# Block sums of the MLPs' second weights: by VectorE from SBUF tiles, or by adding transfers in HBM

## The chip, the core and the metric

One core of a Trainium2 chip runs the whole program. The metric is the device time of one execution in microseconds. The engines are TensorE (PE, and PEld for its weight loads), VectorE (DVE), ScalarE (ACT), GpSimd (POOL) and SyncE (SP); sixteen DMA engines serve the transfers that SP and GpSimd issue.

## What is computed

A decoder trunk of two layers over 512 tokens of width 1024, all in fp32. Layer 0 mixes tokens with a Mamba-2 SSD mixer, layer 1 with HGRN2. After each mixer stand a LayerNorm, an MLP with squared ReLU, a second LayerNorm and a gated per-layer input:

```python
h = layer_norm(ALPHA * x + mix, ln_g[i, 0], ln_b[i, 0])
h = layer_norm(ALPHA * h + sq_relu_mlp(h, w1[i], w2[i]), ln_g[i, 1], ln_b[i, 1])
x = h + sigmoid(h @ ple_w_gate[i]) * (p[i] @ ple_w_proj[i])

def sq_relu_mlp(h, w1, w2):
    a = relu(h @ w1)
    return (a * a) @ w2          # 512x1024 @ 1024x4096, 512x4096 @ 4096x1024
```

## The kernel before

**Split products.** Every fp32 factor is split in two parts, hi and lo, and `mm3` issues three matmuls per product (L120, L121, L122). A weight tile of 512 KB, 128 rows of 1024 columns, is a unit. `unit` loads it on SP's queue into one of three `raw` buffers (L106) and calls `split`: ScalarE casts it into one of six `whi` buffers (L113), and VectorE subtracts that into one of six `wlo` buffers (L116). A raw buffer comes free after L116, a whi and a wlo buffer when TensorE has used them.

**The start.** Eight slots, each a piece of x and of the first weights (512 KB), are loaded first (L161). ScalarE and VectorE split them (L167 to L172), and TensorE takes slot after slot, twelve 512-column matmuls each (L749, then L120 to L122).

**The mixers.** In the SSD mixer (to about 355 us of the span) sixteen pairs of heads each project two weight units; `xz` ends with a Silu on ScalarE (L849). `core` loads rows of cumulated decays from a small HBM tensor, csd (L855), makes a matrix of decays of them (L888 to L892), and TensorE uses it in `diagonal` (L906). The HGRN2 mixer lies at about 820 to 1005 us; its `qf` makes a sigmoid per head on ScalarE (L1074).

**The MLPs.** The hidden units of one MLP come in four groups of 1024. `hidden` computes a group: each step T of a period is a projection by one unit of w1, and `half_blocks` (L300) makes from the result a 2x2 grid of blocks and four signed sums of them, each split in hi and lo. `block_product` multiplies the grid with the 2x2 grid of w2's blocks in seven products in place of eight (Strassen's scheme): three take a plain block of w2, four take a sum t1 to t4 of blocks. Each product is a step Q of a period: two units, 24 matmuls, then a drain of the PSUM banks into `acc` by VectorE (L373 to L379). PERIODS (L32) is the order of T and Q.

**The sums of w2's blocks.** `weight_sums` loads blocks of w2 on GpSimd's queue into eight `r` buffers (L329), and VectorE adds and subtracts them in place (L336 to L344): t3 is d - b, t1 is b - a, t2 is t3 + a, t4 is c - t2, with blocks a, b, c, d. `split` then works on the r tiles. The layer's value and gate projections (`values4`) use the same function for other weights, and the last gate (`last_gate`) already makes its sums with copies and adding transfers into SBUF on GpSimd's queue (L401 to L408).

**Order.** The Tile framework's scheduler orders each engine's instructions by priority and dependence; a lead (LEAD, SUMS) moves a load forward. On each engine, and on each queue, instructions then stand in one fixed row: what waits holds up all behind it. GpSimd does little besides the loads of r and a few memsets.

Of the kernel before, what the change touches and what calls it, by code (L numbers as in the profile page):

```python
# [32 lines left out]
SUMS = (60, 300, 300, 300)  # L33
# [11 lines left out]
def trunk(ctx: ExitStack, tc, a):  # L45
# [184 lines left out]

    def transpose_split(src, dst, c, apart, keep=None):
# [68 lines left out]
    def half_blocks(blk, z0, z1, p):  # L300
# [46 lines left out]
    def block_product(w, blk, lead, first, after=None, turns=None, sums=None, low=None):  # L347

        t1, t2, t3, t4 = weight_sums(w, lead, after=low)
# [3 lines left out]
        def product(x, f, name, start, i, j, turns=None):  # L355
            us = [split(v) if f in (t1, t2, t3, t4) else unit(v) for v in f]
# [3 lines left out]
            for c in range(2):  # L360
# [10 lines left out]
                with tc.high_priority(offset=SOON if after else 0):  # L371
                    if after and f in (w[1][0], t1, t4, w[1][1]):
                        nc.vector.tensor_tensor_reduce(  # L373
                            d, ps, d, 1.0, 0.0, ALU.add, ALU.add, sums[:, 2 - 2 * i + c, j : j + 1]
                        )
# [182 lines left out]
    def mlp_and_gate(layer, h_s, last):  # L558
# [36 lines left out]
        for g, period in enumerate(PERIODS):  # L595
            if g < 4:
                tiles = hidden(g)
            if g > 0:
# [10 lines left out]
                products = block_product(w, blocks.pop(g - 1), SUMS[g - 1], g == 1, *((after, turned(0), sums) if g == 4 else ()), low=low if g == 1 else None)  # L609
# [5 lines left out]

        x_n = Split(8)
# [25 lines left out]
        for h in range(2):  # L642
            pu = unit(a[f"wp_{layer}"][h])
            gu = [unit(a[f"wg_{layer}"][4 * h + j]) for j in range(4)]
            for c in range(NCH):
# [17 lines left out]
                nc.scalar.activation(sg, pg, AF.Sigmoid)  # L663
# [6 lines left out]
        return x_n, rows, late  # L670
# [170 lines left out]
    def xz(j):  # L841
        ps = projected(10 * (j // 4) + 2 + 2 * (j % 4))
        xs = tmp("xs", [P, T])
        conv_silu(ps, j, xs)
        if j == 1:
            toks.extend(dt_tail())
        ps = projected(10 * (j // 4) + 3 + 2 * (j % 4))
        sz = tmp("sz", [P, T])
        nc.scalar.activation(sz, ps, AF.Silu)  # L849
        return xs, sz  # L850
# [112 lines left out]

    pend = None
# [41 lines left out]
    x_s, rows, late = mlp_and_gate(0, h_s, False)  # L1006
# [53 lines left out]
    def qf(h):  # L1060
# [13 lines left out]
        nc.scalar.activation(f, ps[1], AF.Sigmoid)  # L1074
# [389 lines left out]
```

## Time and profile before

| | |
|---|---|
| median of 3 runs | 1412.2 us (1411.4 to 1412.49) |
| span of the profiled execution | 1409.6 us |
| what the median has beside the span | 2.6 us |
| TensorE busy | 1404.3 us |
| VectorE busy | 1069.1 us |
| ScalarE busy | 763.6 us |
| moved by DMA | 181.69 MB, 129 GB/s in the mean |

The profiled execution's own time is not listed apart from its span. A row of a window gives, for each engine, busy us and the count of its instructions, then the clock granted to TensorE, the mean busy share of the sixteen DMA engines and GB/s. A row of a wait view gives engine, line and what ended the wait, then the sum of us, the count and the longest. A row of a timeline gives start, duration, engine, line, operation and tiles, and in brackets the idle time before it. A row of DMA issues gives a count, KB each and the median us from issue to landing.

### The profile page before, as it was taken

The page shows a single profiled execution, that of the slowest core. Times are in us where ns is not written, and L with a number is a line of the kernel's source. Part 1 is how long each engine was busy: PE and PEld are TensorE (multiplying, and loading weights), DVE is VectorE, ACT ScalarE, POOL GpSimd, SP SyncE. Part 2 cuts the span into 40 slices and gives each one's busy share as a digit, 9 for nine tenths or more (in the row PEclk, how much of TensorE's full clock was granted, in tenths as well). Part 3 has the DMA queues.
Part 4 walks back from the last instruction along what each step waited for, and adds up shares of the span by engine and source line. Part 5 has one row for each costly group of instructions (what it writes and reads, how often), then busy time and mean ns, then how long its engine had stood idle before and what let it go on. Part 6 is the DMA issues. An engine that isn't in the chain of part 4 may idle for free.

```text
span 1409.6 us, 20400 instructions
## 1 busy us (share of the span) xinstructions
PE 1404.3 (100%) x8001; PEld 1168.1 (83%) x8001; DVE 1069.1 (76%) x1778; ACT 763.6 (54%) x1156; POOL 45.8 (3%) x92
## 2 busy tenths in 40 slices
PE   9999999999999999999999999999999999999998
PEld 7888888888988888888888888888898888888887
DVE  7989688698977668677986577678785867667795
ACT  7766465573354444545555547655555454544573
POOL 0000000001000000000000000000100000000100
PEclk9999999999999999999999999999999999999999
DMA  8433333234433444345621421222443444444731
GB/s 313 135 117 120 106 120 110 85 100 156 141 113 127 157 131 152 129 142 178 209 90 49 134 91 61 76 87 96 150 135 105 147 137 148 144 137 159 202 106 60
DMA packets 50399, 181.69 MB, mean 129 GB/s; under 512 B 5632, under 2 KB 6400, under 8 KB 50176
## 3 DMA queue, kind: packets, MB, share of 16 engines
q1 hardware_dynamic: 38784, 138.45, 29.6%
q0 software_dynamic: 11520, 41.95, 9.2%
q8 instruction: 63, 1.03, 0.3%
q14 instruction: 32, 0.26, 0.1%
HBM read 177.16 MB, written 2.16 MB: 127 GB/s over the span
## 4 chain that ended last, share of the span: by engine, by line
PE 99%; DMA 0%; DVE 0%; issue 0%; DVEq 0%
PE pj L120 25%; PE pj L121 25%; PE pj L122 25%; PE py L120 5%; PE py L122 5%; PE py L121 5%; PE py L906 1%; PE pt L238 1%; PE py L1175 1%; PE pm L923 1%; PE pm L871 1%; PE py L1301 1%; PE pt L859 0%; PE py L1303 0%; PE py L1240 0%; PE py L832 0%
## 5 line engine op out<-in xcount | busy, mean ns | idle before, releaser
L113 ACT CAST whi<-raw 128x1024 fp32r<-128x1024 f32 x218 | 228.8, 1050 | 333.2 <-PE pj L121 243.6
L120 PE MATMUL pj<-b,whi 128*128 128x512 f32 (+1 forms) x990 | 378.6, 383 | 0.0
L122 PE MATMUL pj<-b,wlo 128*128 128x512 f32 (+1 forms) x990 | 376.8, 381 | 0.0
L121 PE MATMUL pj<-b,whi 128*128 128x512 f32 (+1 forms) x990 | 376.6, 381 | 0.0
L116 DVE TENSOR_TENSOR wlo<-raw,whi 128x1024 fp32r<-128x1024 f32 x218 | 265.4, 1221 | 129.4 <-ACT whi L113 128.2
L121 PEld LDWEIGHTS pj<-b,whi 128*128 128x128 f32 x990 | 186.4, 188 | 34.6 <-issue 0.9
L122 PEld LDWEIGHTS pj<-b,wlo 128*128 128x128 f32 x990 | 186.3, 188 | 34.5
L120 PEld LDWEIGHTS pj<-b,whi 128*128 128x128 f32 x990 | 186.1, 188 | 34.0
L122 PE MATMUL pj<-whi,b 128*128 128x512 f32 x520 | 204.1, 392 | 0.0
L120 PE MATMUL pj<-whi,b 128*128 128x512 f32 x508 | 202.1, 398 | 0.0
L121 PE MATMUL pj<-wlo,b 128*128 128x512 f32 x508 | 199.2, 392 | 0.0
L113 ACT CAST whi<-r 128x1024 fp32r<-128x1024 f32 x76 | 80.0, 1053 | 68.5 <-PE pj L122 39.4
L122 PEld LDWEIGHTS pj<-whi,b 128*128 128x128 f32 x520 | 97.7, 188 | 20.1
L120 PEld LDWEIGHTS pj<-whi,b 128*128 128x128 f32 x508 | 95.5, 188 | 19.1 <-ACT b L1322 0.3
L121 PEld LDWEIGHTS pj<-wlo,b 128*128 128x128 f32 x508 | 95.5, 188 | 18.7 <-issue 0.2
L116 DVE TENSOR_TENSOR wlo<-r,whi 128x1024 fp32r<-128x1024 f32 x76 | 92.5, 1220 | 19.6 <-ACT whi L113 19.1
L122 PE MATMUL py<-whi,b 128*128 128x512 f32 x260 | 101.3, 390 | 0.0
L121 PE MATMUL py<-wlo,b 128*128 128x512 f32 x248 | 96.6, 389 | 0.0
L120 PE MATMUL py<-whi,b 128*128 128x512 f32 x248 | 96.4, 390 | 0.0
L329 POOL DMA_DIRECT2D r<-in_w x64 | 34.0, 532 | 1098.8 <-DVE wlo L116 544.3
L122 PEld LDWEIGHTS py<-whi,b 128*128 128x128 f32 x260 | 48.8, 188 | 10.2
L800 DVE SCALAR_TENSOR_TENSOR cv<-pj,cst,cv 128x509 f32<-128x509 f32 (+2 forms) x66 | 48.9, 746 | 10.6 <-ACT cv L797 9.8
(368 smaller groups left out, 1943.5 us busy)
## 6 DMA issues: line engine op xcount, KB each, us to landing
raw<-in_w SPq DMA_DIRECT2D x112, 512.0 KB, 3.3
r<-in_w POOLq DMA_DIRECT2D x64, 512.0 KB, 3.8
raw<-in_wssd SPq DMA_DIRECT2D x36, 512.0 KB, 3.9
a<-csd SPq DMA_DIRECT2D x16, 512.0 KB, 4.1
raw<-in_wso SPq DMA_DIRECT2D x16, 512.0 KB, 3.3
raw<-in_whq SPq DMA_DIRECT2D x16, 512.0 KB, 3.4
raw<-in_wg SPq DMA_DIRECT2D x15, 512.0 KB, 4.0
raw<-in_whvg SPq DMA_DIRECT2D x14, 512.0 KB, 3.4
```

The source lines that it names most:

```text
L113: nc.scalar.copy(hi[:, :n], f)
L116: nc.vector.tensor_sub(lo[:, :n], f, f32(hi[:, :n]))
L120: nc.tensor.matmul(out, sh, mh, start=start, stop=False, **kw)
L121: nc.tensor.matmul(out, sh, ml, start=False, stop=False, **kw)
L122: return nc.tensor.matmul(out, sl, mh, start=False, stop=stop, **kw)
L238: nc.tensor.transpose(pt[:, j * P : (j + 1) * P], src[:, k * P : (k + 1) * P], ident)
L329: queue.dma_start(t[i][u], src)
L800: nc.vector.scalar_tensor_tensor(cv[:, d:], ps[:, : T - d], convw[:, i, k : k + 1], cv[:, d:], ALU.mult, ALU.add)
L871: nc.tensor.matmul(pst_[:, c * P : (c + 1) * P], btok[:, c, :], xw[:, c].rearrange("p h q -> p (h q)"), start=True, stop=True)
L906: mm = nc.tensor.matmul(yds[0][64 * r : 64 * r + 64, sl], xdt[:, 2 * c + r, :], m[:, r, sl], start=True, stop=True)
L923: mm = nc.tensor.matmul(yo[:, c * P : (c + 1) * P], pv[:, c - 1].rearrange("p h q -> p (h q)"), cm[:, c * P : (c + 1) * P], start=True, st ...
L1175: nc.tensor.matmul(pcs[r][bs, at : at + n], kk[r][:, ts], qs, start=True, stop=True)
```

## The change

The sums of w2's blocks are no longer made by VectorE. Two HBM tensors, s2_0 and s2_1, hold them. `mlp_sums` has 16 steps per layer, four per group, each of two transfers of 1 MB on GpSimd's queue; a transfer is a copy or an add onto what lies in the destination. `start_sums` issues one step behind a given ScalarE instruction: the first transfer of a step gets a dependence on it, the second has only those of its data. For layer 0 the steps hang on the 16 Silus of `xz`, for layer 1 on the 8 sigmoids of layer 0's gate and the 8 of `qf`. `block_product` loads the sums with `unit`, like plain weights. As a transfer can add but not subtract, t1, t2, t3 and t4 become plain sums, and signs move into `half_blocks` and into the drains.

```diff
-SUMS = (60, 300, 300, 300)
...
+    def mlp_sums(layer):
+        w, s = a[f"w2_{layer}"], a[f"s2_{layer}"]
+        rows = lambda v: v.rearrange("u p n -> (u p) n")
+        for g in range(4):
+            wa, wb, wc, wd = (rows(w[8 * g + 2 * i : 8 * g + 2 * i + 2]) for i in range(4))
+            t1, t2, t3, t4 = (rows(s[8 * g + 2 * i : 8 * g + 2 * i + 2]) for i in range(4))
+            yield [(t1, wb, False), (t3, wb, False)]
+            yield [(t1, wa, True), (t3, wd, True)]
+            yield [(t2, t3, False), (t2, wa, True)]
+            yield [(t4, t2, False), (t4, wc, True)]
+
+    def start_sums(steps, ins):
+        for n, (out, src, add) in enumerate(next(steps, ())):
+            dma = nc.gpsimd.dma_start(out, src, accum_op=ALU.add, max_dma_last_dim=8192) if add else nc.gpsimd.dma_start(out, src)
+            if n == 0:
+                tc.add_manual_dep(
+                    dma.ins, ins.ins.name, mybir.DependencyInfo(mybir.DependencyClass.Sync, mybir.DependencyReason.DATA), reason="pace"
+                )
...
-        nc.vector.tensor_add(a22, a21, a22)
+        nc.vector.tensor_sub(a22, a22, a21)
         put("a12", a12)
         nc.vector.tensor_sub(a21, a11, a21)
-        nc.vector.tensor_sub(a11, a22, a11)
-        nc.vector.tensor_sub(a12, a12, a11)
+        nc.vector.scalar_tensor_tensor(a11, a22, -1.0, a11, ALU.mult, ALU.subtract)
+        nc.vector.scalar_tensor_tensor(a12, a12, -1.0, a11, ALU.mult, ALU.subtract)
...
-        t1, t2, t3, t4 = weight_sums(w, lead, after=low)
+        t1, t2, t3, t4 = t
...
-            us = [split(v) if f in (t1, t2, t3, t4) else unit(v) for v in f]
+            us = [unit(v) for v in f]
...
+                    op = ALU.subtract if j else ALU.add
+                    if after and x in ("a12", "s1", "a22", "s4"):
+                        sm_ = sums[:, 2 - 2 * i + c, j : j + 1]
+                        if j:
+                            nc.vector.scalar_tensor_tensor(d, ps, -1.0, d, ALU.mult, ALU.add, accum_out=sm_)
+                        else:
+                            nc.vector.tensor_tensor_reduce(d, ps, d, 1.0, 0.0, ALU.add, ALU.add, sm_)
                     elif (i, j) in seen:
-                        nc.vector.tensor_add(d, ps, d)
+                        nc.vector.tensor_tensor(d, d, ps, op)
                     else:
-                        nc.vector.scalar_tensor_tensor(d, d, ALPHA, ps, ALU.mult, ALU.add)
+                        nc.vector.scalar_tensor_tensor(d, d, ALPHA, ps, ALU.mult, op)
...
+                t = [[a[f"s2_{layer}"][8 * g - 8 + 2 * i + u] for u in range(2)] for i in range(4)]
...
+        steps = mlp_sums(1)
...
-                nc.scalar.activation(sg, pg, AF.Sigmoid)
+                start_sums(steps, nc.scalar.activation(sg, pg, AF.Sigmoid))
...
-        nc.scalar.activation(sz, ps, AF.Silu)
+        start_sums(steps, nc.scalar.activation(sz, ps, AF.Silu))
...
+    steps = mlp_sums(0)
...
-        nc.scalar.activation(f, ps[1], AF.Sigmoid)
+        start_sums(steps, nc.scalar.activation(f, ps[1], AF.Sigmoid))
...
+    for i in range(2):
+        args[f"s2_{i}"] = nc.dram_tensor(f"s2_{i}", (32, P, D), F32).ap()
```

**GpSimd's queue at the start of the program**, before: memsets, then the loads of the first MLP's blocks into r tiles (in_w2_0 is w2 of layer 0).

```order
L187 MEMSET one_23_169 128x1
L189 MEMSET ones_s_24_171 128x64
L329 DMA r_665_3840<-in_w2_0 128x1024
L329 DMA r_659_3834<-in_w2_0 128x1024
L329 DMA r_661_3836<-in_w2_0 128x1024
L329 DMA r_666_3841<-in_w2_0 128x1024
```

The same place now, with the semaphores that each waits for (Activation is ScalarE's, DMASW those of transfers on GpSimd's own queue; 16x16384 is a copy in 16 pieces of 64 KB, 128x2048 an add in 128 pieces of 8 KB):

```order
L188 MEMSET ones_s_24_171 128x64
L245 DMA s2_0<-in_w2_0 16x16384 x2
L245 DMA s2_0<-in_w2_0 16x16384 [waits Activation_49]
L245 DMA s2_0<-in_w2_0 128x2048 [waits DMASW0_49]
L245 DMA s2_0<-in_w2_0 128x2048 [waits DMASW2_49,Activation_49]
L245 DMA s2_0<-s2_0 16x16384 [waits DMASW3_49,Activation_49]
```

Two copies, second transfers of two steps, stand right behind the memsets without a wait; the third transfer is the first that waits for a Silu.

**GpSimd's queue around layer 0's gate and the entry to HGRN2**, before: the last loads for values4, then memsets of two tiles of scores.

```order
L329 DMA r_1074_6342<-in_whvg 128x1024
L329 DMA r_1076_6344<-in_whvg 128x1024
L329 DMA r_1077_6345<-in_whvg 128x1024
L329 DMA r_1078_6346<-in_whvg 128x1024
L1022 MEMSET sc_1132_6662 128x512
L1022 MEMSET sc_1133_6663 128x512
```

Now:

```order
L349 DMA r_1078_6362<-in_whvg 128x1024 [waits DMASW3_49]
L245 DMA s2_1<-in_w2_1 16x16384 [waits DMASW4_49]
L245 DMA s2_1<-in_w2_1 16x16384 [waits DMASW5_49]
L245 DMA s2_1<-in_w2_1 128x2048 [waits DMASW6_49,DMASW4_49]
L245 DMA s2_1<-in_w2_1 128x2048 [waits DMASW7_49,DMASW5_49]
L245 DMA s2_1<-in_w2_1 16x16384 [waits DMASW0_49,Activation_49]
L245 DMA s2_1<-s2_1 16x16384 [waits DMASW1_49,Activation_49]
L245 DMA s2_1<-in_w2_1 128x2048 [waits DMASW2_49,DMASW0_49]
L245 DMA s2_1<-in_w2_1 128x2048 [waits DMASW3_49,DMASW1_49]
L245 DMA s2_1<-in_w2_1 16x16384 [waits Activation_49]
L245 DMA s2_1<-s2_1 16x16384 [waits DMASW3_49]
```

The steps of layer 1 now lie between values4's loads and the memsets of the scores; what the gate's sigmoids do not pace stands close behind values4's loads.

**SP's queue in the first MLP**, before: units of w1 and of w2's plain blocks.

```order
L106 DMA raw_717_4194<-in_w1_0 128x1024
L106 DMA raw_725_4260<-in_w1_0 128x1024
L106 DMA raw_728_4310<-in_w2_0 128x1024
L106 DMA raw_731_4316<-in_w2_0 128x1024
L106 DMA raw_743_4357<-in_w1_0 128x1024
```

Now the sums' units stand among them:

```order
L105 DMA raw_692_4070<-in_w1_0 128x1024
L105 DMA raw_695_4101<-s2_0 128x1024
L105 DMA raw_698_4107<-s2_0 128x1024
L105 DMA raw_704_4142<-in_w1_0 128x1024
L105 DMA raw_707_4174<-s2_0 128x1024
L105 DMA raw_710_4180<-s2_0 128x1024
```

All loads of an MLP's weights now share this queue and its three raw buffers. TensorE's row keeps all its instructions; only transposes near the MLPs' second norms stand some matmuls earlier or later.

More of the change, by code (lines that the diff above doesn't have):

```diff
@@ L345, in weight_sums, with block_product @@
         return t
-    def block_product(w, blk, lead, first, after=None, turns=None, sums=None, low=None):
-        t1, t2, t3, t4 = weight_sums(w, lead, after=low)
+    def block_product(w, t, blk, first, after=None, turns=None, sums=None):
+        t1, t2, t3, t4 = t
         seen = set() if first else {(i, j) for i in range(2) for j in range(2)}
@@ L669, in mlp_and_gate @@
                 late.append(lambda h=h, c=c: turn(h, c))
-        return x_n, rows, late
+        return x_n, rows, late, steps
     def values4(xs, rows, late):
@@ L1005, in trunk @@
     begin("mlp0")
-    x_s, rows, late = mlp_and_gate(0, h_s, False)
+    x_s, rows, late, steps = mlp_and_gate(0, h_s, False)
     made = {}
```

6 lines of the change are left out of this document (1 added, 5 removed).

## The prediction

> **What bounds the kernel now.** I read the list of cores and the page's first part, then what TensorE waits for, then windows inside the first MLP beside a few rows of its timeline.
>
> ```profile
> core 0: 1409.6 us, clock 1.000
> PE 1404.3 (100%) x8001; PEld 1168.1 (83%) x8001; DVE 1069.1 (76%) x1778; ACT 763.6 (54%) x1156; POOL 45.8 (3%) x92
> PE pm L153 <- PEq L1452: 0.8, 1, 0.8
> PE py L749 <- DVE b L167: 0.6, 1, 0.6
> 438.01 0.39 PE L120 MATMUL pj<-whi,b 128*128 128x512 f32 x1
> 438.24 0.39 PE L121 MATMUL pj<-wlo,b 128*128 128x512 f32 x1
> 420.00:500.00 80.00, 80.00 (x355) 66.24 (x354) 57.63 (x68) 40.11 (x50) 4.24 (x8) 1.00 0.43 136
> 500.00:600.00 100.00, 100.00 (x443) 82.81 (x442) 68.77 (x81) 47.19 (x58) 5.29 (x10) 1.00 0.43 141
> ```
>
> The two wait rows are all that the view of waits lists for TensorE: 1.4 us, both before its first real matmul. Busy alone would not prove a full pipe, since the ends of matmuls are modelled. The starts do: two 512-column matmuls start 0.23 us apart, and 443 of them in 100 us is one per 0.226 us. In the MLPs, where the change takes work off VectorE, TensorE issues at its own pace, at the full granted clock. So the kernel is bound by TensorE from 4.7 us on, and there is no wait for a lighter VectorE to remove. What can move the time is a new wait.
>
> **The change part by part.** *VectorE's sums* (L336 to L344) go:
>
> ```profile
> L339 DVE TENSOR_TENSOR r<-r,r 128x1024 f32<-128x1024 f32 x18 | 22.0, 1223 | 16.4 <-DMA r<-in_w 16.2
> L340 DVE TENSOR_TENSOR r<-r,r 128x1024 f32<-128x1024 f32 x18 | 22.0, 1220 | 0.2
> L336 DVE TENSOR_TENSOR r<-r,r 128x1024 f32<-128x1024 f32 x18 | 21.9, 1224 | 30.8 <-DMA r<-in_w 30.8
> L344 DVE TENSOR_TENSOR r<-r,r 128x1024 f32<-128x1024 f32 x18 | 21.9, 1223 | 11.1 <-DMA r<-in_w 10.5 <-DVE wlo L116 0.4
> L223 DVE SCALAR_TENSOR_TENSOR acc<-acc,lnmv,a 128x1024 f32<-128x1024 f32 x16 | 20.4, 1278 | 0.1
> ```
>
> Of each row's 18, 16 are the MLPs' (8 blocks, 2 halves; 2 are values4's and stay): 64 instructions by 1.22 us, 78 us of VectorE. On the path they are worth 0. The signs turned in half_blocks make 32 plain operations into scalar_tensor_tensor; 1278 against 1220 ns at 1024 columns makes some 0.03 us at 512, 1 us in all, under the same cover. The drains with a subtraction cost what they did.
>
> *Loads of the sums* move from GpSimd's queue and eight r buffers to SP's queue and three raw buffers, 8 units a block. What is late next there would be a raw tile:
>
> ```profile
> SPq L106 <- DVE wlo L116: 911.6, 183, 26.4
> ACT whi L113 <- PE pj L121: 250.9, 85, 5.5
> raw<-in_w SPq DMA_DIRECT2D x112, 512.0 KB, 3.3
> L113 ACT CAST whi<-raw 128x1024 fp32r<-128x1024 f32 x218 | 228.8, 1050 | 333.2 <-PE pj L121 243.6
> ```
>
> SP waits for raw buffers and the cast waits for TensorE to give back whi: the loads run ahead as far as buffers let them, up to six split units. The densest stretch, the seven products at an MLP's end, takes two units per 24 matmuls (5.4 us). Three raws turn around in 3.3 us of landing, 1.05 of cast, 1.22 of subtraction and 0.45 of issue (1.80 for the four of L161, below), about 6.0 us for three units against 8.2 us that TensorE needs for them. I take 0; without that cover each late unit would cost up to 2 us, and I keep 2 us for the top of the range. Around the MLPs' norms the scheduler put transposes up to some 16 matmuls elsewhere; TensorE waits nowhere there now: 0, ends -1 and +1.
>
> *The sums in HBM* are 64 transfers of 1 MB on GpSimd's queue: 32 copies, 32 adds. Only the first of each step waits for ScalarE. In GpSimd's order the first two copies, second transfers of their steps, wait for nothing and stand right behind the last memset:
>
> ```profile
> 0.96 0.15 POOL L189 MEMSET ones_s<- 128x64 f32 x1
> 0.74 1.80 SPq L161 DMA_DIRECT2D acc<-in_xw  x4
> 2.00:4.00 2.00, 2.00 (x6) 1.38 (x5) 0.00 (x0) 0.02 (x1) 0.00 (x0) 1.00 0.93 360
> 12.00:16.00 4.00, 4.00 (x26) 3.06 (x28) 3.99 (x8) 3.04 (x7) 0.00 (x0) 1.00 1.03 402
> 4.17 0.71 ACT L171 CAST whi<-acc 128x256 fp32r<-128x256 f32 x2 [2.15 <-DMA acc<-in_xw]
> 7.29 0.62 ACT L167 CAST b<-acc 128x512 fp32r<-128x512 f32 x1 [0.72 <-DMA acc<-in_xw]
> r<-in_wg POOLq DMA_DIRECT2D x1, 512.0 KB, 3.6
> 1330.50:1332.50 2.00, 2.00 (x11) 1.65 (x9) 1.41 (x4) 0.03 (x1) 0.00 (x0) 1.00 1.03 416
> 1334.80:1338.30 3.50, 3.50 (x17) 2.92 (x16) 2.64 (x6) 1.22 (x4) 0.00 (x0) 1.00 0.99 191
> ```
>
> From 2 to 16 us (0.93 in the first 2 us of it, full in the last 4) the DMA engines are busy with the loads that start TensorE. GpSimd is free at 1.1 us. A plain load on its queue (in 1304:1308) lands in 3.6 us, of which 512 KB at 416 GB/s are 1.3, so the copies' first bytes can stand in the queues 1.1 to 3.4 us into the span, while slot 0 is under way (360 GB/s brings its 512 KB to about 3.3 us). The 1330 window is one copy from last_gate, the 1334 window one of its adds, alone at a full share: 416 and 191 GB/s. A 1 MB copy is then 2.5 us of all engines, an add 5.5 us. No row has a copy from HBM to HBM; its bounds are 2.5 us and, if it is as slow as the add, 5.5. I take 2.5, since a copy does no arithmetic. Each piece is 64 KB, one per engine, and I expect it to be moved whole: two copies hold the start back by 5.0 us (up to 11).
>
> The Trainium skill ("DMA: Bandwidth & Descriptors", Latency and other measured facts) gives 214 GB/s per direction for copies between HBM tensors at full rate; by that, as an estimate, a copy is 4.9 us and the sum below comes to 1423.5. No run here has shown one yet.
>
> *Later steps of the first layer.*
>
> ```profile
> L849 ACT ACTIVATE sz<-pj x16: 578/582/599, 29.7 to 316.6; 128x512 f32<-128x512 f32 x16
> 29.70:316.60 286.90, 286.90 (x1587) 239.97 (x1586) 235.53 (x457) 175.44 (x235) 0.00 (x0) 1.00 0.35 115
> a<-csd SPq DMA_DIRECT2D x16, 512.0 KB, 4.1
> 45.82 3.78 SPq L855 DMA_DIRECT2D a<-csd  x2
> 52.72 1.22 DVE L892 TENSOR_TENSOR b<-b,cbm 128x1024 f32<-128x1024 f32 x1
> 56.10 1.09 PE L906 MATMUL py<-b,xdt 128*64 128x128 f32 x16
> ```
>
> 14 copies by 2.5 and 16 adds by 5.5 make 123 us in 287, 0.43 of the engines beside 0.35 now: room, and weights have the six units' cover (6 by 5.4 = 33 us). The thinner cover is the decay rows: csd tiles land in 4.1 us, and the first heads' chain ends at 53.9 us, 2.2 us before TensorE takes it at 56.1. An add in front of one of them would cost at most 5.5 - 2.2 = 3.3 us there, and nothing where the cover is longer; 0 to 3.3, I take 1.0.
>
> *The second layer's first half.* In the order of GpSimd's queue (section on the change) its steps wait for the gate's eight sigmoids:
>
> ```profile
> L663 ACT ACTIVATE sg<-pj x8: 591/598/599, 713.7 to 760.9; 128x512 f32<-128x512 f32 x8
> 726.00:820.00 94.00, 94.00 (x426) 77.54 (x425) 59.09 (x72) 53.75 (x70) 1.28 (x4) 1.00 0.32 99
> ```
>
> Six copies and six adds are 48 us of engines, with 0.32 of 94 us already used (30): 78 of 94. values4's r loads stand ahead of them and would have landed long before. GpSimd may now wait in front of scs' memsets, and raws land later beside the adds: 0 to 2, I take 0.5.
>
> **Sum.** 5.0 + 1.0 + 0.5 = 6.5 us: a span of 1409.6 + 6.5 = 1416.1. The median of the runs shown, 1412.2, is 2.6 above the profiled span; 1416.1 + 2.6 = 1418.7 us.
>
> **The rivals.** *The start is shared, not blocked (ends not slower).* If the engines take turns in small pieces, loads go at half speed from about 2.4 us on; slot 0 is late by 0.9 us and each next by 1.3 more. Splitting runs ahead of TensorE by more each slot:
>
> ```profile
> 6.69 0.68 DVE L172 TENSOR_TENSOR wlo<-acc,whi 128x512 fp32r<-128x512 f32 x1
> 7.59 0.39 PE L120 MATMUL py<-b,whi 128*128 128x512 f32 x1
> 8.55 0.68 DVE L172 TENSOR_TENSOR wlo<-acc,whi 128x512 fp32r<-128x512 f32 x1
> 9.87 0.69 DVE L172 TENSOR_TENSOR wlo<-acc,whi 128x512 fp32r<-128x512 f32 x1
> 10.31 0.39 PE L120 MATMUL py<-b,whi 128*128 128x512 f32 x1
> DMA packets 50399, 181.69 MB, mean 129 GB/s; under 512 B 5632, under 2 KB 6400, under 8 KB 50176
> ```
>
> Slot 1 has 0.2 us to spare (7.59 - 7.37), slot 2 1.1 (10.31 - 9.23), slot 3 2.5 (10.31 plus the 2.72 of a slot, less 10.56); the delay is the largest of 0.9, 2.2 - 0.2, 3.5 - 1.1 and 4.8 - 2.5: 2.4 us. With nothing lost later, 1414.6, inside 0.2% (2.8 us, about what a measurement of this kernel can tell from no change). It decides if the granule is under about 16 KB, or if the copies come later than slot 3. Against it: 223 packets of 8 KB and more are in the page, so long pieces are moved as such. The Trainium skill (same page, SWDGE vs HWDGE vs iDMA) has packets of preferably no more than 4096 B as the boundary at which an engine changes queues, which would be this rival; the 223 speak against a strict limit. Chance 0.18.
>
> *The mixers' DMA saturates (much slower).* If adds in HBM take twice the 5.5 us, since the old value comes from HBM as well, and copies 5.5, the steps take 14 by 5.5 plus 16 by 11 = 253 us of 287, beside 0.35 (100): 66 us too many. GpSimd can run on into the MLP's eight hidden units before the first sums are wanted (43 us at 5.4 each), so I let half of it reach TensorE, 33 us; with 11 at the start, 1456. For it: no row bounds an add into HBM from above. Against: 33 us of units in reserve. Chance 0.06.
>
> *A lighter VectorE helps (faster).* Only TensorE's waits could shrink: 1.4 us in all, none behind VectorE in the MLPs. At most 1412.2 - 1.0 = 1411.2, not to be told from no change; by over 0.2% chance 0.03.
>
> **How the numbers follow.** Forecast 0.73, shared start 0.18, saturation 0.06, faster 0.03. Slower is 0.73 + 0.06 = 0.79, within 0.2% 0.18, faster 0.03. The range runs from the shared start with 2 us less, 1412.6, to the start at 11 with 3.3 for csd and 2 for late units, 1412.2 + 16.3 = 1428.5, rounded to 1428; it leaves out saturation and the faster tail.
>
> **What would show it.** Right: two copies on GpSimd at about 1.1 us, the first cast of slot 0 or 1 late by about 5 us, TensorE's first L120 row or the slots behind it late by as much, and no wait of TensorE in the MLPs. Of the shared start: a first cast near 5 us and 2 to 3 us lost. Of saturation: a DMA share near 1.00 from 30 to 320 us and matmuls further than 0.23 us apart there. Wrong altogether: a start as before, or an MLP with fewer than 443 matmuls in 100 us.

## The result, and the profile after

The changed kernel takes 1446.9 us in the median of four executions (1443.9 to 1452.8), the kernel before 1412.0 beside it: 1.0247 of the time, 95% interval 1.0219 to 1.0274. That is 35 us slower, where 6.5 were forecast. The profiled execution took 1449.9 us, 1.8 of it outside the span.

The cores, the totals and the packets of the page after:

```profile
core 0: 1448.1 us, clock 0.991
PE 1416.4 (98%) x8001; PEld 1175.0 (81%) x8001; DVE 999.4 (69%) x1714; ACT 764.2 (53%) x1156; POOL 55.6 (4%) x92
DMA packets 56034, 248.82 MB, mean 172 GB/s; under 512 B 6657, under 2 KB 7425, under 8 KB 51201
```

VectorE lost 64 instructions and 69.7 us, as meant, and TensorE does the same 8001 matmuls. They now wait: the span is 31.7 us over TensorE's busy time, where it was 5.3, and busy time itself has grown by 12.1 us at a lower mean clock. Packets of 8 KB and more went from 223 to 4833: 512 pieces of 64 KB from the copies, 4096 of 8 KB from the adds, and the old ones.

What TensorE waits for, after; the two rows of this view before came to 1.4 us:

```profile
PE pt L882 <- ACT xs L824: 7.8, 1, 7.8
PE pm L946 <- DVE pv L905: 5.5, 1, 5.5
PE pt L258 <- DVE b L263: 3.8, 1, 3.8
PE pt L258 <- DVE acc L223: 3.4, 2, 2.2
PE py L119 <- ACT whi L170: 2.5, 1, 2.5
PE py L121 <- DVE b L705: 1.9, 1, 1.9
```

There are few waits, and they are long. Their releasers are small steps of ScalarE and VectorE that take 1 us, so what counts is what stood ahead of those. The chain of waits says it (start, us, what was in the way):

```profile
4.70 15.47 DMA b<-in_xw
...
38.69 12.60 DMA raw<-in_wssd
51.42 0.84 issue
52.26 0.64 ACT xs L824
...
302.58 19.51 DMA raw<-in_wso
322.12 1.05 ACT whi L112
...
388.73 9.08 DMA raw<-in_w
397.89 1.04 ACT whi L112
...
678.63 4.90 DMA raw<-s
...
792.52 9.87 DMA raw<-in_lmask
```

Ahead of the long waits a load lands 9 to 20 us after its issue. The medians have moved little (in_w 3.4 after 3.3, in_wssd 4.6 after 3.9): the loss is in a few loads.

Since both kernels run the same matmuls in nearly the same order, the start of the k-th in one trace can be set against the k-th in the other. The growth of that difference, by stretches of the kernel before (us), is a ledger of where the time went. Here it is for all kernels that follow; it is worked out from the matmuls' starts, one profiled execution each. That execution can lie some us from the median (e3's 4.9 above it, e13's 5.0 below). The row of e7, where every engine turned out to have the changed kernel's order of instructions, shows how far a stretch moves from one execution to the next: up to some 3 us.

```
us of the kernel before   0-30 30-100 100-300 300-350 350-420 420-650 650-730 730-900 900-end   all
after the change           3.8   10.0     0.0     7.8     6.3     0.0     5.0     4.1     1.5  38.5
e1_no_transfers            0.0    0.2     0.0     0.0     4.0     0.0     2.1     0.0     0.3   6.7
e2_transfers_alone         3.4    8.5     0.0    10.1     3.9     9.6     0.4     5.9     0.1  41.9
e3_both_paced              0.8    6.7     0.1     6.6     0.0     0.0     4.8    18.0     1.6  38.5
e4_signs_alone             0.0    0.0     0.0     0.0     0.0     0.0     0.5     0.0     0.1   0.6
e5_sums_in_r               5.0    7.3     0.0     7.1    10.3     0.0     1.2     7.1     0.0  38.1
e6_paced_small             0.8   11.1     0.0     0.0     3.0     0.0     2.9     0.0     1.9  19.7
e7_values_held             5.4    7.5     0.0     7.4     6.9     0.0     1.9     6.0     1.4  36.5
e8_late_casts              6.0    8.0     8.4     8.5     6.6     0.0     2.0     3.9     1.0  44.5
e9_casts_held              6.3    0.7    15.0    24.9     6.7     0.0     2.8     6.0     1.0  63.4
e12_held_no_transfers      1.1    0.7     1.0     3.8     2.7     0.0     1.6     0.0     1.1  12.1
e10_small_copies          -0.1    5.9     0.0     0.0     2.7     0.0     2.1     8.3     1.6  20.5
e11_all_cures              2.2    2.1    11.6     6.5     0.0     0.0     0.4     0.7     0.0  23.5
e13_small_and_r            0.0    4.0     0.0     0.0     0.0     0.0     0.0     0.2     0.1   4.2
e14_later_start            1.0    0.4     0.0     0.0     0.0     0.0     1.4     0.8     0.0   3.6
```

In the row after the change, the start lost 3.8 us, about what was forecast. The mixer's next two places lost 17.8, the first MLP's first norm (350 to 420) 6.3, the MLPs' ends 6.5 (650 to 730, and 900 to the end, where all of it falls near 1350), the second mixer's start 4.1.

The first large loss, in ScalarE's timeline after (start, us, then the idle time before it):

```profile
40.31 1.06 ACT L112 CAST whi<-raw 128x1024 fp32r<-128x1024 f32 x1 [0.68 <-DMA raw<-in_wssd]
51.31 1.05 ACT L112 CAST whi<-raw 128x1024 fp32r<-128x1024 f32 x1 [9.94 <-DMA raw<-in_wssd]
52.26 1.15 ACT L824 ACTIVATE xs<-cv 128x512 f32<-128x512 f32 x2
```

and the same place before, with its waits of ScalarE for DMAs:

```profile
38.09 1.05 ACT L113 CAST whi<-raw 128x1024 fp32r<-128x1024 f32 x1 [1.93 <-DMA raw<-in_wssd]
39.05 1.15 ACT L801 ACTIVATE xs<-cv 128x512 f32<-128x512 f32 x2
ACT whi L113 <- DMA raw<-in_wssd: 8.2, 3, 4.3
ACT whi L113 <- DMA raw<-in_w: 4.5, 4, 1.8
```

ScalarE takes its instructions in a fixed order. The cast at 51.31 us is of a unit that TensorE first uses at 83.0 us (by the order of the program and the starts in the trace). xs, which TensorE wants at 45 us, is ready to be computed and stands behind that cast. Up to 420 us ScalarE's order is the same in both traces; what changed is when the load lands. TensorE's units are far ahead; ScalarE's order is not. The row before shows it too: ScalarE already stood 1.93 us for this load, so on this path the cover was nothing.

### The profile page after: what moved, and what is told of

It reads as the page before. It is cut to its first block, busy times and chain, and to the rows that moved or that the text cites. A ratio compares the mean times of both kernels' runs of the same rounds, so it can differ in the third digit from the quotient of the medians.

```text
span 1448.1 us, 20509 instructions
## 1 busy us (share of the span) xinstructions
PE 1416.4 (98%) x8001; PEld 1175.0 (81%) x8001; DVE 999.4 (69%) x1714; ACT 764.2 (53%) x1156; POOL 55.6 (4%) x92
## 4 chain that ended last, share of the span: by engine, by line
PE 84%; DMA 7%; DVE 6%; ACT 2%; issue 1%; SPq 0%; ACTq 0%; DVEq 0%
PE pj L119 22%; PE pj L120 22%; PE pj L121 22%; PE py L121 4%; PE py L120 4%; PE py L119 4%; DVE wlo L115 2%; DMA raw<-in_w 2%; DMA raw<-in_wso 1%; ACT whi L112 1%; DMA raw<-s 1%; DMA b<-in_xw 1%; PE py L929 1%; PE pt L258 1%; DMA raw<-in_wssd 1%; PE py L1199 1%
## 5 line engine op out<-in xcount | busy, mean ns | idle before, releaser
L115 DVE TENSOR_TENSOR wlo<-raw,whi 128x1024 fp32r<-128x1024 f32 x282 | 344.0, 1223 | 272.2 <-ACT whi L112 271.7
L112 ACT CAST whi<-raw 128x1024 fp32r<-128x1024 f32 x282 | 296.8, 1053 | 423.5 <-PE pj L120 241.0
L245 POOL DMA_DIRECT2D s<-in_w x48 | 35.7, 763 | 759.8 <-ACT sg L686 365.6
L121 PEld LDWEIGHTS py<-whi,b 128*128 128x128 f32 x260 | 48.8, 188 | 12.6 <-DVE b L705 2.3
L119 PEld LDWEIGHTS py<-whi,b 128*128 128x128 f32 x248 | 46.5, 188 | 10.6 <-DVE acc L398 0.6
L120 PEld LDWEIGHTS py<-wlo,b 128*128 128x128 f32 x248 | 46.6, 188 | 9.5
```

Of the source, the lines that this page charges most:

```text
L112: nc.scalar.copy(hi[:, :n], f)
L115: nc.vector.tensor_sub(lo[:, :n], f, f32(hi[:, :n]))
L119: nc.tensor.matmul(out, sh, mh, start=start, stop=False, **kw)
L120: nc.tensor.matmul(out, sh, ml, start=False, stop=False, **kw)
L121: return nc.tensor.matmul(out, sl, mh, start=False, stop=stop, **kw)
L245: dma = nc.gpsimd.dma_start(out, src, accum_op=ALU.add, max_dma_last_dim=8192) if add else nc.gpsimd.dma_start(out, src)
```

## The experiments

Theory from these views: transfers make weight loads late, and a late load blocks ScalarE's order. Rivals: the new signs and drains; the three raw buffers; the place of the other instructions, whatever the transfers do.

**e1_no_transfers.** `start_sums` iterates over nothing, and the MLPs load plain blocks where the sums were:

```
-            for n, (out, src, add) in enumerate(next(steps, ())):
+            for n, (out, src, add) in enumerate(()):
-                t = [[a[f"s2_{layer}"][8 * g - 8 + 2 * i + u] ...
+                t = [[w2[8 * g - 8 + 2 * i + u] ...
```

> The 64 transfers are left out, and the MLPs load plain blocks of w2 in place of the sums (the MLPs' results differ for it); signs, drains and loads through raw stay as changed. The theory: by the two traces laid side by side along TensorE's instructions, 31.9 of the 38.5 us that the changed kernel lost lie where transfers run (start 3.8, at 50 us 10.0, at 310 us 7.8, at 380 us 6.3, at 780 us 2.2, at 840 us 1.8), because weight loads land late behind them and ScalarE's casts, which wait for them in its fixed order, hold up what TensorE needs next. Then this run takes 1412 + 6.6, 1417 to 1420 us, and keeps the losses at the ends of the MLPs (4.8 and 1.4 us). The rival: the MLPs' loads through three raw buffers are the cost everywhere; then it stays over 1435 us.

1418.1 us, 1.0041 of before [1.0027, 1.0055]. Without transfers 29 of the 35 us are gone, and all of the mixers' losses. What is left is not from the transfers: 4.0 us in the first norm and 2.1 at the first MLP's end. In the norm VectorE does this:

```profile
377.76 1.27 DVE L223 SCALAR_TENSOR_TENSOR acc<-acc,lnrs,b 128x1024 f32<-128x1024 f32 x1
378.95 1.22 DVE L356 TENSOR_TENSOR r<-r,r 128x1024 f32<-128x1024 f32 x1
380.08 0.68 DVE L263 TENSOR_TENSOR b<-pt,b 128x512 fp32r<-128x512 f32 x1
```

L356 is a sum for values4, which comes more than 300 us later. The r buffers are free now, so its loads are early, and the sum lands in the middle of the norm's chain. On the chain of waits it takes 1.1 us there. TensorE's two waits come to 1.8 us, and its clock is halved behind them from 382.6 to 386.0 us, which takes another 1.7. That the early sums are the cause of the whole 4.0 is inferred: e4 and e13, where they lie elsewhere, lose 0.0.

**e2_transfers_alone.** The kernel before, with the 64 transfers added and their results not used; VectorE goes on making the sums:

```
+        start_sums(steps, nc.scalar.activation(sz, ps, AF.Silu))
-        nc.scalar.activation(sz, ps, AF.Silu)
```

> The kernel before with the 64 transfers added and their sums not used: VectorE still makes the sums from r tiles. The theory (transfers in front of weight loads): about 1412 + 32, 1437 to 1450 us, with the losses at the start and near 50, 310 and 380 us, none at the ends of the MLPs. The rival (loads through raw): 1412 to 1418 us.

1454.9 us, 1.0303 [1.0286, 1.0321]. The transfers alone cost all of the loss and more; the mixers' entries are near those after the change. The 9.6 at 420 to 650 are its own: the first MLP's r loads stand among the steps on GpSimd's queue and land by 398.1 us, but VectorE's order has their sums only at 459 to 482 us, right before a cast that TensorE waits 7.3 us for. At the MLPs' ends it loses 0.5, so the 6.5 there need the sums' way through the raw buffers.

**e3_both_paced.** Both transfers of a step wait for the pacing instruction, so nothing is issued at the start:

```
-            if n == 0:
+            if True:
```

> As the changed kernel, but both transfers of a step wait for its ScalarE instruction, so no copy runs in the first 30 us. The theory: the start's 3.8 us are gone and the rest stays, 1443 us (1440 to 1446). The rival: the two copies only move to the crowded stretch after the first Silu and cost as much there, 1447 us or more.

1445.0 us, 1.0236 [1.0217, 1.0256]. The start's 3.8 fall to 0.8, and the first norm's 6.3 to 0.0. After the change, eight of the second layer's transfers that no sigmoid paces are issued before 391 us, the last four in the norm (the view merges the first two; a fourth follows at 390.52):

```profile
377.77 0.99 POOL L245 DMA_DIRECT2D s<-in_w  x2 [2.03 <-issue]
388.14 0.87 POOL L245 DMA_DIRECT2D s<-in_w  x1 [9.38 <-DMA s<-in_w]
```

The load of 388.73 us, 9.08 in the chain above, stands behind these; in e3 the second layer's first transfer is issued at 732.7. Yet the time does not fall. Those transfers now come later, seven of them are issued from 757.9 to 776 us ahead of lmask's load, and 18.0 us are lost at 730 to 900, where the chain of waits has

```profile
778.52 20.98 DMA raw<-in_lmask
```

**e4_signs_alone.** No transfers; VectorE makes plain sums as before and the new signs and drains use them:

```
+        t1, t2, t3, t4 = t = plain_sums(w, t, after=low)
```

> No transfers; VectorE makes the plain sums t1 to t4 from r tiles as before, with the changed signs in half_blocks and in the drains. If the losses at the ends of the MLPs (4.8 and 1.4 us) come of sums that are loaded through three raw buffers, this is the time before, 1412 us (within 1.5). The rival: they come of the signs, of the drains with a subtraction, or of the transposes' other places; then 1417 to 1419 us.

1412.3 us, 0.9998 [0.9989, 1.0008]. Signs and drains cost nothing.

**e5_sums_in_r.** The sums are loaded into the eight r buffers instead of the three raw ones:

```
+            r = tmp("r", [P, 1024])
+            nc.sync.dma_start(r, src)
-            us = [unit(v) for v in f]
+            us = [spare(v) if f in (t1, t2, t3, t4) else unit(v) for v in f]
```

> The sums are loaded into the eight r buffers, which the changed kernel no longer fills in the MLPs, instead of through the three raw buffers; all else is as after the change. Theory (the three raw buffers, emptied by ScalarE, do not turn around fast enough for the twice as many loads of the MLPs' last thirds): the stalls at the two MLP ends, 6.2 us of the ledger (4.8 at 670-710 us and 1.4 at 1350 us), go to under 1.5; and since r is occupied again, the second value product's sums move back behind the first MLP, which gives back up to 4 us at 380-390 us. Together about 1437 to 1441 us. Rival (the loads are late because of what the queues or the DMA engines carry, and the buffers do not matter): the stalls at the MLP ends stay at 4 us or more, and the time within 2 us of 1446.9 unless the part at 380-390 us alone goes (1443).

1449.8 us, 1.0266 [1.0248, 1.0283]. In time a miss. In the ledger the MLPs' ends fall from 6.5 to 1.2, as expected of the buffers. The first norm does not get better but worse, 10.3. Eight loads of sums, issued from 356 to 379 us, are under way there and take 20 to 26 us, and the load ahead of the norm lands late like the others:

```profile
386.56 13.35 DMA raw<-in_w
```

**e6_paced_small.** As e3_both_paced, with pieces of 4 KB:

```
-            dma = nc.gpsimd.dma_start(out, src, accum_op=ALU.add, max_dma_last_dim=8192) if add else nc.gpsimd.dma_start(out, src)
+            dma = nc.gpsimd.dma_start(out, src, accum_op=ALU.add, max_dma_last_dim=4096) if add else nc.gpsimd.dma_start(out, src, max_dma_last_dim=4096)
```

> As e3_both_paced (each of a step's two transfers waits for the pacing instruction), with copies and adding transfers cut to pieces of 4 KB. Theory (size of the pieces: a load's 4 KB piece stands behind a piece of 64 KB, 2.5 us, or of 8 KB, 0.65 us, on each DMA engine): landings that took 12 to 20 us come down, the stalls at 40-80 us and at 310 us (6.7 and 6.5 us in e3_both_paced) at least halve, and so does the one at 780 us (15.6); the time is about 1425 to 1435 us. Rival (what counts is the total that the adding transfers keep the DMA engines busy, in whatever pieces): the stalls stay within 2 us each of those of e3_both_paced and the time at 1443 to 1450 us. A third way: the smaller pieces make the transfers themselves slower, so that they reach into the next step's: over 1450 us.

1427.1 us, 1.0107 [1.0088, 1.0125]: 18 us less than e3_both_paced for the same bytes. GpSimd's order changed with the pieces, so the 18 us are not the pieces' alone. The losses at 300 to 350 and 730 to 900 are gone. Before 100 us they are not, by the same blocked order:

```profile
44.57 1.04 ACT L112 CAST whi<-raw 128x1024 fp32r<-128x1024 f32 x1 [6.94 <-DMA raw<-in_wssd]
45.52 1.15 ACT L824 ACTIVATE xs<-cv 128x512 f32<-128x512 f32 x2
```

**e7_values_held.** values4's sums wait until the first MLP's norm is done:

```
+        lows.append(low)
-        t1, t2, t3, t4 = weight_sums(w, VALUE_SUMS)
+        t1, t2, t3, t4 = weight_sums(w, VALUE_SUMS, after=lows[0])
```

> As after the change, with the sums of the second value product's weights on VectorE held back until the first MLP's first norm has been computed. Theory (those sums stand in VectorE's order in the middle of the norm, because the buffers r are free so early): the loss at 380-390 us, about 4 us without transfers and 1.5 us in the changed kernel's own ledger beyond its weight wait there, goes; the time is 1441 to 1445 us. Rival (the place of these sums does not matter when the transfers are there, since the norm waits for weights in any case): within 1 us of 1446.9.

1449.3 us, 1.0252 [1.0223, 1.0282]: no gain, and my reason was wrong. After the change these sums do not stand in the norm at all; VectorE's order has them at 550 us, where none waits (their loads were issued by 375.7 us):

```profile
L356 DVE TENSOR_TENSOR r<-r,r x2: 1220/1221/1222, 550.4 to 556.3; 128x1024 f32<-128x1024 f32 x2
```

So the edit moved nothing: on every engine the order of instructions is the changed kernel's, and this run is a second measurement of it. The 6.3 us in the norm are a late weight load; the sums stand there in e1, e6 and e10.

**e8_late_casts.** The mixer's casts get a lead of 50 in place of 100:

```
-        return split(raw[:, :n], lead, after)
+        return split(raw[:, :n], cast or lead, after)
-        project(unit(wssd[i - 4]), x_s, ps)
+        project(unit(wssd[i - 4], cast=50), x_s, ps)
```

> As after the change, with the casts and subtractions of the SSD mixer's weight units given a lead of 50 steps of the program instead of 100 in the scheduler's order; their loads are issued as early as before. Theory (a late landing costs TensorE because the cast that waits for it stands in ScalarE's order ahead of what TensorE needs next): with the casts further back the waits at 53 us (7.8 us) and at 310 to 325 us (about 8 us) shrink to under a third, and the time is 1430 to 1438 us. Rival (the landing itself is too late for the matmuls that need the unit): the waits move to TensorE's own wait for the cast and stay within 2 us in sum; the time is 1444 to 1450 us.

1450.1 us, 1.0263 [1.0211, 1.0315]. This tells nothing: in ScalarE's order the cast at 310 us kept its place, and at 50 us one cast moved by one instruction. Why the smaller lead moved so little was not tested; perhaps the scheduler sets a cast by when it thinks that the load has landed.

**e9_casts_held and e12_held_no_transfers.** Here the casts are tied to a later place; e12 is the same without transfers:

```
+            with behind(hold):
+                nc.scalar.copy(hi[:, :n], f)
-        project(unit(wssd[i - 4]), x_s, ps)
+        project(unit(wssd[i - 4], hold=uses.get(i - HOLD)), x_s, ps)
-                units = [unit(w[2 * h + i]) for i in range(2)]
+                units = [unit(w[2 * h + i], hold=decayed[0] if h else None) for i in range(2)]
```

> As after the change, with the casts of the SSD mixer's weights tied to a later place in ScalarE's order: a projection's cast stands behind ScalarE's use of the projection three units earlier, and the casts of the second half of an output projection behind the decays of the current step. e8 had left these casts ahead of what TensorE waited for at both places; this moves them behind it, with TensorE's first matmul on them still over 10 us away. Theory (a late landing costs time because its cast stands in ScalarE's fixed order ahead of an operation that TensorE needs first): the waits at 53 us (10.0 of the ledger) and at 310 us (7.8) fall to under 3 us each, the rest of the ledger stays, and the time is 1431 to 1437 us if the order costs nothing else. Rival (the landing is too late for TensorE itself, or the three raw buffers, now held longer, make the next loads late): the waits move to other places with 14 us or more in all, and the time is 1443 us or more.

> Control for e9_casts_held: the same order of the casts, without any transfers (the MLPs load plain weight blocks in place of the sums, as in e1_no_transfers). Theory: the later casts cost nothing where the loads are prompt, so the time is that of e1_no_transfers, 1418.1 us, within 1.5 us. Rival (the new order costs time by itself): 1421 us or more, and that much has to be taken off the result of e9_casts_held.

e9 1479.8 us, 1.0478 [1.0443, 1.0513]; e12 1424.6, 1.0092 [1.0077, 1.0107]. At 30 to 100 us the theory holds: 10.0 falls to 0.7, as in the control. In e9's ScalarE timeline the order no longer stands:

```profile
43.02 0.63 ACT L829 ACTIVATE xs<-cv 128x512 f32<-128x512 f32 x1
46.79 0.60 ACT L877 ACTIVATE sz<-pj 128x512 f32<-128x512 f32 x1 [3.13 <-PE pj L126]
47.28 0.62 ACT L829 ACTIVATE xs<-cv 128x512 f32<-128x512 f32 x1
```

As a cure it fails. A held cast keeps its raw buffer, the next load is issued later, and further on an unheld cast of the first half of an output projection blocks the order:

```profile
332.93 1.04 ACT L117 CAST whi<-raw 128x1024 fp32r<-128x1024 f32 x1 [12.78 <-DMA raw<-in_wso]
334.00 1.28 ACT L829 ACT_TABLE_LOAD   x1
335.29 0.63 ACT L829 ACTIVATE xs<-cv 128x512 f32<-128x512 f32 x1
```

Each half of the expectation came true at a place, and the ledger's loss went up by 25 us; the later casts by themselves account for some 6 (e12 against e1).

**e10_small_copies.** As e6_paced_small, with the adds back at 8 KB:

```
-accum_op=ALU.add, max_dma_last_dim=4096
+accum_op=ALU.add, max_dma_last_dim=8192
```

> As e6_paced_small, with only the copies cut to 4 KB pieces; the adding transfers keep their pieces of 8 KB. Theory (the copies' pieces of 64 KB, 2.5 us each, are what makes the loads late, the adding pieces of 0.65 us do little): within 3 us of e6_paced_small, 1424 to 1430 us, and no wait at 310 us. Rival (the 8 KB adding pieces do it, which outlast a load's 4 KB piece several times over): the stalls at 310 us (6.5 us) come back and the time is 1436 us or more.

1433.1 us, 1.0143 [1.0119, 1.0167]. Between the two expectations. The loss at 300 to 350 us stays away, so the 8 KB adds did not make that one. Whether the 64 KB copies did is not separated: GpSimd's order is another than in e3, which issues seven transfers from 281 to 301 us where e10 issues four from 279 to 295. Against e6 the comparison is clean, since all engines have the same order: in e10's profile 8.3 us at 730 to 900 are back, and its median is 6 us over e6; the intervals just touch, so a price of 8 KB adds is likely and not settled.

**e11_all_cures and e13_small_and_r.** The edits of e6 and e5 together (e13), and those of e9 as well (e11):

```
-            us = [unit(v) for v in f]
+            us = [spare(v) if f in (t1, t2, t3, t4) else unit(v) for v in f]
-            if n == 0:
+            if True:
...
+            with behind(hold):
+                nc.scalar.copy(hi[:, :n], f)
```

> All that helped together: pieces of 4 KB and both transfers of a step paced (e6_paced_small), the sums loaded into the eight r buffers (e5_sums_in_r), the SSD mixer's casts held (e9_casts_held). Theory (each stall has its own cause, and they add): of the ledger of e6_paced_small, 19.7 us, the part at 50 to 80 us (11.1) falls to under 4, the parts at the MLP ends (4.7) to under 2, and the part at 380 us (3.4) stays: 1414 to 1420 us, still not under the kernel before, since VectorE's sums cost it nothing. Rival (the cures get into each other's way, or the transfers cost a floor that no order avoids): 1422 us or more.

> As e11_all_cures without the held casts: pieces of 4 KB, both transfers of a step paced, sums loaded into the eight r buffers; the casts stand as after the change. Theory (small pieces and the r buffers cure different stalls and add; the held casts cost 6.5 us by themselves and more with transfers): of e6_paced_small's ledger the parts at 380 us (3.4) and at the MLP ends (4.7) go to under 1 each, the part before 100 us (11.9) stays, and the time is 1418 to 1423 us. Rival (the gain at 380 us and at the MLP ends in e11_all_cures came with its later loads, not with the r buffers): those parts keep 4 us or more in all, 1424 us or more.

e11 1435.6 us, 1.0167 [1.0152, 1.0182]; e13 1420.5, 1.0062 [1.0045, 1.0079]. The held casts are the harm (18.1 of e11's 23.5 at 100 to 350). Small pieces and r buffers add: the first norm is at 0.0 and the MLPs' ends at 0.1 in e13. r, once occupied, also puts values4's sums back to 684 us. Nine executions of e13 spread from 1415.5 to 1427.9, and the profile is of the fastest; its loss lies before 100 us.

**e14_later_start.** As e13_small_and_r, with no step in the first four z tiles and some later tiles starting two:

```
+        for _ in range((0, 0, 0, 0, 2, 1, 2, 1, 1, 2, 1, 1, 2, 1, 1, 1)[j]):
+            start_sums(steps, ins)
```

> As e13_small_and_r, with the first layer's sixteen steps begun only at the fifth of the sixteen z tiles (none at tiles 0 to 3, then two steps at tiles 4, 6, 9 and 12 and one at the others). Theory (what is left is the first 100 us alone, where the loads have no lead yet; in the steady mixer small pieces are hidden): the ledger before 100 us falls from 10 or more to under 2, the double steps cost under 3, and the time is 1412 to 1415.5 us, not under the kernel before. Rival (two steps at once bring the stalls back elsewhere in the mixer): the ledger between 100 and 330 us grows by as much as the start loses, 1418 us or more.

1412.8 us, 1.0003 [0.9993, 1.0012]: as fast as before, not faster. Its window of the mixer (after the name of a window: busy us of the engines, clock, DMA share, GB/s), and the same stage after the change:

```profile
100.00:317.00 217.00, 217.00 (x1195) 181.35 (x1194) 173.05 (x334) 128.09 (x170) 19.43 (x27) 1.00 0.84 236
```

```profile
33.00:330.00 297.00, 283.75 (x1552) 237.03 (x1550) 230.45 (x441) 170.98 (x228) 19.10 (x28) 0.98 0.70 206
```

With the DMA engines busy 0.84 of the time TensorE loses nothing; at 0.70, after the change, it loses 18 us. So the mean share was not the matter. Nor are large pieces enough for a loss. Most of the mixer after the change has them and loses nothing:

```profile
100.00:310.00 210.00, 210.00 (x1160) 175.67 (x1159) 165.79 (x314) 122.43 (x161) 14.51 (x21) 1.00 0.67 193
```

Ten of the 30 weight loads issued from 100 to 300 us took 9 to 21 us to land (the longest was 5.0 before), and TensorE did not wait once. What fits both is that a late landing costs only where its cast has no time to spare in ScalarE's order.

## Why the prediction was wrong

**The bound, VectorE's sums, signs and drains: right.** TensorE's pace in the MLP is what it was, with a lighter VectorE beside it:

```profile
448.00:548.00 100.00, 100.00 (x443) 82.80 (x442) 60.28 (x75) 49.33 (x62) 0.00 (x0) 1.00 0.44 139
```

The sums were worth 0 within the measurement, as e14 shows: the work is off VectorE and the time the same to 0.1%. 64 by 1.22, 78 us, overstates the 69.7 that went, since consecutive records overlap by some 0.1 us (in e1, 378.95 + 1.22 is past the next start, 380.08). Signs and drains: 0, e4.

**The start: right.** 5.0 forecast, 3.8 in this profile, 3.4 to 6.3 in e2, e5, e7, e8 and e9, and -0.1 to 2.2 where both transfers are paced.

```profile
1.37 1.17 POOL L245 DMA_DIRECT2D s<-in_w  x2 [0.26 <-issue]
5.91 0.62 ACT L170 CAST whi<-acc 128x512 fp32r<-128x512 f32 x1
12.41 0.62 ACT L166 CAST b<-acc 128x512 fp32r<-128x512 f32 x1 [5.88 <-DMA acc<-in_xw]
4.75:10.60 5.85, 5.83 (x23) 4.81 (x24) 2.56 (x5) 1.30 (x3) 0.00 (x0) 1.00 0.99 396
```

The cast that came at 7.29 us comes at 12.41, 5.1 late: two copies of 2.5 us, in pieces moved whole. The packet records show it: 16 pieces of 64 KB start at 4.75 to 5.0 us and 16 more at 7.5 to 7.9, each 2.4 to 2.8 us long. SP's queue starts some 30 pieces of 4 KB between the two, from 7.18 to 7.71, and otherwise none from 4.9 to 9.9. The 214 GB/s of the Trainium skill ("DMA: Bandwidth & Descriptors", Latency and other measured facts), measured on tiles with rows of 16 KiB from other queues, would have made these two copies 9.8 us; the trace does not agree, and has 5.1.

**Later steps of the first layer: here it failed.** The step said "weights have the six units' cover (33 us)" and took 1.0 us for the decay rows. It measured 10.0 + 7.8 (7.5 + 7.4 in e7). The cover is TensorE's: the unit cast at 322.1 us is first used at 356.7. But the cast of a unit has a place in ScalarE's order, and from there the cover is the time from landing to that cast; before, it was below nothing in the rows above (ScalarE waited for in_wssd three times, 8.2 us). The experiments bear this out at 30 to 100 us: without transfers 0.2 are lost (e1), with the casts held back 0.7 (e9). At 310 us holding casts back did not help (24.9 in e9), and there the chain of waits is the evidence. The decay rows, which I did watch, are not in the waits. Nor did the share of 0.43 + 0.35 help: the measured 0.70 is near it, and no measure of how late one load is.

**The loads of the sums: too small a term.** 0 was taken, with 2 us for the top of the range; 6.5 were lost at the MLPs' ends, 3.3 in e7 and 2.4 without transfers (e1). With eight more buffers they are 0.1 to 1.4 (e5, e11, e13, e14). So three raws did not turn around in 6.0 us. On the chain there, landings of 4.6 to 5.8 us stand in place of the 3.3 that I used:

```profile
692.36 5.82 DMA raw<-s
...
702.33 4.58 DMA raw<-in_w
709.32 5.11 DMA raw<-in_w
```

The sums in HBM are not what delays these: GpSimd issues no transfer from 391 to 746 us. The loads there are issued about every 2 us (698 to 712 us), so two or three are under way at once. The 6.0 also left out that casts and subtractions queue with ScalarE's and VectorE's other work.

**The second layer's transfers: too small, and one place missing.** For its first half 0.5 was taken (0 to 2), 4.1 measured; the late load there is lmask's, 9.87 us in the chain above. The prediction had its steps wait for the gate's sigmoids, with values4's loads ahead of them. Eight of them waited for none, four of these stood even ahead of values4's loads, and the last four ran in the norm, from 377.8 to 404 us. The sum has no term for them; the first norm lost 6.3, and 0.0 when they were paced (e3).

**Not seen at all:** TensorE's clock, below, some 9 us of the 38.5; and values4's sums, which move into the first norm once r is free (4.0 us in e1; after the change they stand at 550 us and cost nothing there).

**The rivals.** The shared start (turns in small pieces, 2.4 us, nothing later) fell: the copies' pieces were moved whole, and most of the loss came later. Saturation (a share near 1.00 and matmuls further apart all through) is not what happened, though the 1446.9 lie near its price: TensorE runs at full pace between a few long waits, and an add of 1 MB, eight pieces of 0.63 us for each engine, is 5.0 us and not the 11 that it assumed. That its time comes near is chance. Nothing shows a gain from a lighter VectorE.

What stays open: how much of the 12 us between e10 and e3, and of the 18 between e6 and e3, is the pieces' size and how much GpSimd's order, which changed with it; and the price of 8 KB adds.

## What to carry to other kernels

A prefetch's cover has to be counted on every engine that touches the load in order, not only at the last user: the waits of ScalarE for DMAs were the place to look. Background transfers are judged by how late they make one load, against the time to spare at that place, and not by their mean share of the DMA engines; their start, their pacing and probably their piece size set that. A pace put on the first of two transfers leaves the second free to run far ahead. And work taken off an engine that nothing waits for gives nothing back, even when the transfers that replace it are made free.

## What the hardware showed beside

**Pieces.** A copy between HBM tensors in pieces of 64 KB keeps a DMA engine 2.6 us for each in the median (2.4 to 4.1, packet records of the trace). An 8 KB adding piece takes 0.63 us in the median. From 41 to 48 us 118 of these start and 127 load pieces of 4 KB, about one for one, so that loads get some 75 GB/s of their usual 400. The Trainium skill ("DMA: Bandwidth & Descriptors", Queues, rings and completion order) says that an engine drains a whole packet of one queue before it turns to another; the start agrees. The Trainium skill's same page (Bandwidth, Measured) advises transfers of 1 MiB and more for the rate; e6 moves the same 1 MB transfers, cut into smaller packets and in another order, and gains 18 us over e3.

**The clock after a wait.** TensorE's timeline behind the wait at 320 to 326 us, and the window (clock third from the end):

```profile
326.02 1.62 PE L946 MATMUL pm<-cm,pv 128*128 128x128 f32 x6 [5.46 <-DVE pv L905]
327.29 0.77 PE L121 MATMUL pj<-b,wlo 128*128 128x512 f32 x1
327.87 0.63 PE L119 MATMUL pj<-b,whi 128*128 128x512 f32 x1
328.29 0.63 PE L120 MATMUL pj<-b,whi 128*128 128x512 f32 x1
327.29:330.43 3.14, 3.14 (x10) 2.46 (x10) 2.75 (x6) 1.70 (x4) 0.00 (x0) 0.50 1.00 402
```

The granted clock is 0.50, and matmuls start some 0.42 us apart instead of 0.23, until 330.4 us: at half pace 4.4 us of work take 2.2 more, and with the wait of 5.5 that is the 7.8 of the ledger. The waits of 7.8 us at 53 us, 3.8 at 400 and 2.2 at 730 had it too:

```profile
400.20:405.00 4.80, 4.80 (x23) 4.80 (x24) 3.30 (x5) 0.88 (x2) 0.00 (x0) 0.50 0.62 165
```

The trace's clock records put the halved stretches at 50.53 to 57.36, 323.60 to 330.42, 398.69 to 405.52 and 729.78 to 733.20 us. All lengths and distances are multiples of 3.41 us. Half of what lies in them after the waits (4.4, 4.4, 5.3 and 3.3 us) is some 9 us of the 38.5. The Trainium skill ("TensorE: Matmul & The Clock Gate", Part 1) has the clock halved after about 3.4 us without work, by a window that runs free of the program. The halved clock and the steps of 3.41 us agree. That it takes some 3.4 us without work does not: the wait of 2.15 us at 730 was enough, while one of 2.48 us before 13.60 us was not. What decides between these two is open.
